# Time-mixing keys and values as three products of rounded parts instead of one fp32 product

## The chip, the cores and the metric

The kernel runs on one core of a Trainium2 chip. Its time is the device time of one execution in microseconds (us); several runs are taken and their median is given. A core has five engines that work side by side, each through its own queue of instructions in order: TensorE (PE in the profile; its weight loads are PEld) does matrix products into PSUM, VectorE (DVE), ScalarE (ACT) and GpSimd (POOL) do elementwise work, SyncE (SP) mostly issues transfers (DMA). Engines wait for each other through semaphores.

## The reference

It is one inference step of a two-layer decoder in fp32 with 1024 features. The 16 meta tokens, 1024 prompt tokens and 8 decode tokens (one new token in each of 8 sequences) go through layer 0 (a Conformer convolution module), a squared-ReLU MLP of width 4096, layer 1 (RWKV-7 time mixing), another such MLP and a final norm. The change lies in the time mixing:

```python
xx = prev - h                        # prev: the row before
xr, xw, xk, xv, xa, xg = (h + xx * x_mix[i] for i in range(6))
r, k, v = xr @ w_r, xk @ w_k, xv @ w_v          # 1024 x 1024 each
w_log = -softplus(-(w0 + tanh(xw @ w1) @ w2)) - 0.5
a = sigmoid(a0 + (xa @ a1) @ a2);  g = sigmoid(xg @ g1) @ g2
kk = (k * k_k) / norm(k * k_k)       # for each of 16 heads of 64
k = k * (1 + (a - 1) * k_a)
# for each token: S = S * decay + (S @ -kk) (kk * a)^T + v k^T;  y = S r
out = ((groupnorm(y) + sum(r * k * r_k) * v) * g) @ w_o
```

## The kernel before

**Layout.** Activations lie with features on the 128 partitions, in 8 blocks of 128 features (KT = 8), and tokens along the free dimension. The time-mixing stage works on four groups of 272, 256, 256 and 264 tokens (G1, L33).

**Two kinds of dense product.** Outside the time mixing, dense products are made of three products of rounded parts: `mm3` (L185 to L189) adds hi x hi, lo x hi and hi x lo in one PSUM bank. A part is the value rounded to the format fp32r (hi), or what the rounding left (lo). `load_w` splits a weight block of 128x1024 by one copy on ScalarE (L157) and four subtractions of 128x256 on GpSimd (L162); `split` (L138 to L141) does it for activations. In the time mixing the products of r, k and v take fp32 operands directly, one matmul where `mm3` has three.

**Order of a group.** `prepare(g)` (L773) loads the group's normalised rows, subtracts neighbours (L788, two thirds on VectorE, one third on GpSimd) and provides `mix(i, k)` (L808 to L813), one VectorE operation that makes a 128-feature block of one mixed input. `mixer_in(g)` (L822) then runs three loops over 8 column blocks p of 128 output features:

- r (from L927): 8 mixes, then for each p the product (`proj`, L848 to L854: 8 matmuls over the k-blocks), an eviction and a store to HBM;
- the narrow products of the gate (`gate`, `narrow`, L873), then k (from L944): 8 mixes, for each p the product, an eviction (L955), a square for the norm (L958), a small product that sums it (pn, L950) and the gate's second product (l_g, L892) with its eviction;
- the norm of k (`norms`), the narrow products of decay and rate (p_wa), then v (from L1043): 8 mixes, for each p the product and a long elementwise part on VectorE and ScalarE (L1053 to L1096) that reads r and k back from HBM (`fetch`, rk2), and `finish`, with small products (nn L1015, vt L998, pk L1031) and stores.

**Weights.** `col_stream` (L176) gives the 96 weight blocks (4 groups x r, k, v x 8) in the order of use, each loaded on SyncE's queue up to 4 blocks ahead of its use into a pool of 6 raw buffers (L755). Other pools: 4 wide buffers for the narrow weights (L756), 20 for the mixes (L757).

**The recurrence** over 17 chunks (the 16 meta tokens, then 64 tokens each) runs interleaved with these loops. `inverses` (L1124) reads small blocks, does 60 VectorE operations for each burst (L1135, L1136) and stores the result; `front` (A, L1176) and `chunk` (gg, bT, W, po, U, S, Y) are chains of small products with elementwise steps on VectorE, ScalarE and GpSimd (for GpSimd: clearing part of xa, and sw).

**What sets the order.** The program is written in generators: `tick` and `advance` (from L1318) move the recurrence forward by an amount (PACE, L1418) at each half block, `beside` moves the next group's `prepare` forward within v. A scheduler at build time then fixes the order of instructions on each engine, and pools with a set number of buffers add the waits: a tile can be written again only when its last reader is done.

Of the kernel before, what the change touches and what calls it, by code (L numbers as in the profile page):

```python
# [8 lines left out]
F32 = mybir.dt.float32  # L9
# [39 lines left out]
def hybrid_step(tc, x_prompt, x_sample, state_conv, state_shift, state_wkv, meta_tokens,  # L49
# [10 lines left out]
    with ctx:  # L60
        def pool(stack, name, bufs, **kw):
            return stack.enter_context(tc.tile_pool(name=name, bufs=bufs, reuse_waits="tile", **kw))
# [110 lines left out]
        def blocks_of(raw):  # L173
            return raw.rearrange("p (a b) -> p a b", a=KT)

        def col_stream(cols, ahead):  # L176

            raws = {}
            for i in range(len(cols)):
                for j in range(i, min(i + ahead + 1, len(cols))):  # L180
                    if j not in raws:
                        raws[j] = load_raw(col_src(*cols[j][:2]), (KT, P), cols[j][2])
                yield blocks_of(raws.pop(i))

        def mm3(ps, w, act, first, last):  # L185

# [19 lines left out]
        def tt(name, tag):  # L206
            return cur["tmp"].tile([P, cur["n"]], F32, name=name, tag=tag)
# [544 lines left out]
        nc.vector.tensor_scalar(omka, pvec[:, col["k_a"]:col["k_a"] + KT], -1.0, 1.0, op0=ALU.mult, op1=ALU.add)  # L752

        hnp = pool(ld, "hnp", 1)
        cur["raw"] = pool(ld, "wrawd", 6)  # L755
        wide = pool(ld, "wided", 4)  # L756
        mixp = pool(ld, "mixp", 20)  # L757
        lorap = pool(ld, "lorap", 1)
        pr = pool(ld, "pr", 1)
        def open_ep(stack, bufs, tag):  # L760
# [12 lines left out]
        def prepare(g):  # L773
# [33 lines left out]

            def mix(i, k):  # L808

                t = mixp.tile([P, N1], F32, name=nm("mx", i, k), tag="mx")  # L810
                nc.vector.scalar_tensor_tensor(t[:, :n], xx[:, k, :n], vec("x_mix", i * KT + k), hx[:, k, 1:1 + n],
                                               op0=ALU.mult, op1=ALU.add)
                return t[:, :n]  # L813

            prep[g] = mix, hx, sps if npr < n else None

        wrkv = col_stream([(w, p, f"w{s}{g}_{p}") for g in range(4)
                           for s, w in (("r", rwkv_w_r[0]), ("k", rwkv_w_k[0]), ("v", rwkv_w_v[0]))
                           for p in range(KT)], 4)
        carry = {"tail": lambda: None}  # L820

        def mixer_in(g, tick, ahead):  # L822
# [25 lines left out]
            def proj(w, act, wid, name, fill=None):  # L848
                ps = bank(nm("p", name))
                for k in range(KT):  # L850
                    nc.tensor.matmul(ps[:wid, :n], w[:, k, :], act[k], start=k == 0, stop=k == KT - 1)  # L851
                    if fill and k in (2, 5):
                        fill()
                return ps  # L854
# [737 lines left out]
```

## Time and profile before

| | us |
|---|---|
| median of 3 runs | 2863.09 |
| lowest and highest | 2858.82, 2869.78 |
| profiled execution | 2865.08 |
| its span in the profile | 2863.4 |

The mean clock granted to TensorE in the profiled execution was 0.975 of full speed. The time-mixing stage reaches from 1126 to 1850 us of the span. In the profile's rows, L851 is a line of the kernel, "x" counts records, and shapes are partitions x elements; a row of a view by lines ends with the engine's idle time before the group and what ended it. A row of the table by stretches has the start and end, the length, then for each engine its busy time and records, the granted clock, the busy share of the DMA engines and GB/s. In the chain of waits each piece is what the next one waited for. A row of the timeline has start, length, engine, line, operation, names, shapes and count.

### The profile page before, as it was taken

The page shows a single profiled execution, that of the slowest core. Times are in us where ns is not written, and L with a number is a line of the kernel's source. Part 1 is how long each engine was busy: PE and PEld are TensorE (multiplying, and loading weights), DVE is VectorE, ACT ScalarE, POOL GpSimd, SP SyncE. Part 2 cuts the span into 40 slices and gives each one's busy share as a digit, 9 for nine tenths or more (in the row PEclk, how much of TensorE's full clock was granted, in tenths as well). Part 3 has the DMA queues.
Part 4 walks back from the last instruction along what each step waited for, and adds up shares of the span by engine and source line. Part 5 has one row for each costly group of instructions (what it writes and reads, how often), then busy time and mean ns, then how long its engine had stood idle before and what let it go on. Part 6 is the DMA issues. An engine that isn't in the chain of part 4 may idle for free.

```text
span 2863.4 us, 51601 instructions
## 1 busy us (share of the span) xinstructions
PE 2756.3 (96%) x19594; PEld 2553.4 (89%) x19594; DVE 1795.2 (63%) x3618; ACT 1185.9 (41%) x2230; POOL 1436.1 (50%) x1983
## 2 busy tenths in 40 slices
PE   8999999999999899979999999979999999999998
PEld 7999999999999898858778877768889999999998
DVE  5999999995465545167455771679756764443444
ACT  5545444543364332232434643534345552222223
POOL 6677877987788774000000110265448783333332
PEclk9999999999999999989999999989999999999999
DMA  6663544454445643778768785675557742222211
GB/s 177 176 186 88 154 139 133 134 178 140 140 129 149 192 140 120 214 198 197 199 181 217 212 215 150 195 179 149 131 152 215 208 134 86 67 74 67 67 60 41
DMA packets 659270, 428.15 MB, mean 150 GB/s; under 512 B 126840, under 2 KB 609208, under 8 KB 659022
## 3 DMA queue, kind: packets, MB, share of 16 engines
q1 hardware_dynamic: 652780, 421.93, 52.1%
q10 hardware_dynamic: 6018, 2.89, 0.4%
q8 instruction: 155, 2.54, 0.4%
q14 instruction: 93, 0.76, 0.1%
q0 software_dynamic: 224, 0.03, 0.0%
HBM read 353.03 MB, written 72.66 MB: 149 GB/s over the span
## 4 chain that ended last, share of the span: by engine, by line
PE 37%; DVE 7%; POOL 5%; DMA 3%; issue 3%; ACT 1%; SPq 0%; DVEq 0%; POOLq 0%; ACTq 0%
PE ps_in L187 3%; PE ps_in L188 3%; PE ps_in L189 3%; POOL wo_lo L162 3%; PE out L187 3%; PE out L189 3%; PE out L188 3%; PE p_v L851 3%; PE p_k L851 2%; POOL wi_lo L162 2%; PE p_r L851 2%; PE A L1176 2%; DVE ni L1136 1%; DVE tt L1135 1%; PE U L1260 1%
## 5 line engine op out<-in xcount | busy, mean ns | idle before, releaser
L162 POOL TENSOR_TENSOR wo_lo<-wo_raw,wo_hi 128x256 fp32r<-128x256 f32 x736 | 563.4, 799 | 286.3 <-ACT wo_hi L157 267.4
L162 POOL TENSOR_TENSOR wi_lo<-wi_raw,wi_hi 128x256 fp32r<-128x256 f32 x640 | 490.5, 799 | 272.0 <-ACT wi_hi L157 259.7
L187 PE MATMUL out<-hh,wo_hi 128*128 128x352 f32 (+2 forms) x1536 | 502.7, 327 | 18.5 <-DVE h L340 9.3
L187 PE MATMUL ps_in<-m_h,wi_hi 128*128 128x352 f32 (+2 forms) x1536 | 498.8, 325 | 12.3 <-ACT m_h L269 11.5
L340 DVE TENSOR_TENSOR h<-h,out 128x352 f32<-128x352 f32 (+2 forms) x768 | 385.5, 509 | 188.3 <-PE out L189 187.2
L189 PE MATMUL out<-hl,wo_hi 128*128 128x352 f32 (+2 forms) x1536 | 494.8, 325 | 6.8 <-DVE hl L141 6.8
L188 PE MATMUL out<-hh,wo_lo 128*128 128x352 f32 (+2 forms) x1536 | 497.7, 324 | 0.0
L189 PE MATMUL ps_in<-m_l,wi_hi 128*128 128x352 f32 (+2 forms) x1536 | 497.0, 324 | 0.0
L188 PE MATMUL ps_in<-m_h,wi_lo 128*128 128x352 f32 (+2 forms) x1536 | 496.7, 324 | 0.0
L504 DVE SCALAR_TENSOR_TENSOR cv<-u,wdw,cv 128x352 f32<-128x352 f32 (+2 forms) x720 | 376.5, 572 | 0.7
L157 ACT CAST wi_hi<-wi_raw 128x1024 fp32r<-128x1024 f32 x160 | 168.0, 1050 | 396.5 <-PE out L189 189.0
L157 ACT CAST wo_hi<-wo_raw 128x1024 fp32r<-128x1024 f32 x184 | 192.8, 1049 | 311.5 <-PE out L189 144.1
L187 PEld LDWEIGHTS out<-hh,wo_hi 128*128 128x128 f32 x1536 | 292.2, 190 | 26.3 <-DVE h L340 13.7
L187 PEld LDWEIGHTS ps_in<-m_h,wi_hi 128*128 128x128 f32 x1536 | 290.9, 189 | 15.6 <-ACT m_h L269 11.7
L189 PEld LDWEIGHTS out<-hl,wo_hi 128*128 128x128 f32 x1536 | 291.7, 191 | 9.0 <-DVE hl L141 8.1
L188 PEld LDWEIGHTS out<-hh,wo_lo 128*128 128x128 f32 x1536 | 292.2, 190 | 1.3
L188 PEld LDWEIGHTS ps_in<-m_h,wi_lo 128*128 128x128 f32 x1536 | 290.7, 189 | 1.7
L189 PEld LDWEIGHTS ps_in<-m_l,wi_hi 128*128 128x128 f32 x1536 | 290.6, 189 | 1.8
L327 DVE SCALAR_TENSOR_TENSOR r<-ps_in,rs_m 128x352 f32<-128x352 f32 (+2 forms) x192 | 98.5, 515 | 235.7 <-PE ps_in L189 232.0
L141 DVE TENSOR_TENSOR hl<-s,hh 128x352 fp32r<-128x352 f32 (+2 forms) x192 | 143.8, 750 | 112.0 <-ACT hh L140 111.9
L329 ACT ACTIVATE s<-r 128x352 f32<-128x352 f32 (+2 forms) x192 | 93.7, 490 | 141.6 <-DVE r L327 141.3
L851 PE MATMUL p_r<-mx,wr_raw 128*128 128x256 f32 (+2 forms) x512 | 123.4, 396 | 4.1 <-DVE n L1017 4.1
(350 smaller groups left out, 4926.9 us busy)
## 6 DMA issues: line engine op xcount, KB each, us to landing
wi_raw<-in_w_mlp_in_dram SPq DMA_DIRECT2D x160, 512.0 KB, 4.0
wo_raw<-in_w_mlp_out_dram SPq DMA_DIRECT2D x160, 512.0 KB, 3.7
wr_raw<-in_rwkv_w_r_dram SPq DMA_DIRECT2D x32, 512.0 KB, 6.0
wk_raw<-in_rwkv_w_k_dram SPq DMA_DIRECT2D x32, 512.0 KB, 4.2
wv_raw<-in_rwkv_w_v_dram SPq DMA_DIRECT2D x32, 512.0 KB, 4.5
d_ab<-ab SPq DMA_DIRECT2D x32, 512.0 KB, 4.0
pg_raw<-in_conv_w_pw_dram SPq DMA_DIRECT2D x24, 512.0 KB, 4.6
pa_raw<-in_conv_w_pw_dram SPq DMA_DIRECT2D x24, 512.0 KB, 4.7
```

The source lines that it names most:

```text
L141: eng_lo.tensor_sub(lo, src, hi.bitcast(F32))
L157: nc.scalar.copy(hi[:, :a * b], raw[:, :a * b])
L162: eng_lo.tensor_sub(lo[:, cs], raw[:, cs], hi[:, cs].bitcast(F32))
L187: nc.tensor.matmul(ps, w[0], act[0], start=first, stop=False)
L188: nc.tensor.matmul(ps, w[1], act[0], start=False, stop=False)
L189: nc.tensor.matmul(ps, w[0], act[1], start=False, stop=last)
L327: nc.vector.scalar_tensor_tensor(r[:, :n], ps[:, :n], 0.0, rs[:, :n], op0=ALU.max, op1=ALU.mult)
L329: nc.scalar.activation(s[:, :n], r[:, :n], AF.Square)
L340: nc.vector.tensor_add(hv[:, 4 * i + m, :], hv[:, 4 * i + m, :], ps[:, :n])
L504: nc.vector.scalar_tensor_tensor(acc[m][:, :n], ug[:, m, j:j + n], wdw[:, m, j:j + 1], acc[m][:, :n], op0=ALU.mult, op1=ALU.add)
L851: nc.tensor.matmul(ps[:wid, :n], w[:, k, :], act[k], start=k == 0, stop=k == KT - 1)
L1176: nc.tensor.matmul(ps[:, i * 2 * P:(i + 1) * 2 * P], bk[:, j + i, :], xa[:, j + i].rearrange("p q x -> p (q x)"), start=True, stop=True)
```

## The change

In the products of k and v the fp32 matmul is replaced by `mm3`; r keeps its fp32 matmul. For this, `col_stream` splits the blocks of k and v one block ahead of their use, as `load_w` does elsewhere: a copy on ScalarE, four subtractions on GpSimd, into a new pool of two buffers for each part. `mix` for k and v writes to a temporary tile and splits it, the lo part by VectorE for even k-blocks and by GpSimd for odd ones. Pools become smaller: raw 6 to 4 (and the look-ahead 4 to 3), wide 4 to 3, mixes 20 of one kind to 10 of each of two kinds, which r's mixes use in turn.

```diff
-        def col_stream(cols, ahead):
+        def col_stream(cols, ahead, split_ahead):
 
-            raws = {}
+            raws, parts = {}, {}
             for i in range(len(cols)):
                 for j in range(i, min(i + ahead + 1, len(cols))):
                     if j not in raws:
                         raws[j] = load_raw(col_src(*cols[j][:2]), (KT, P), cols[j][2])
-                yield blocks_of(raws.pop(i))
+                for j in range(i, min(i + split_ahead + 1, len(cols))):
+                    if j not in parts:
+                        if not cols[j][3]:
+                            parts[j] = [blocks_of(raws[j])]
+                            continue
+                        hi, lo = (cur["wsp"].tile([P, 8 * P], F32R, name=cols[j][2] + q, tag="w" + q) for q in "hl")
+                        nc.scalar.copy(hi, raws[j])
+                        for c in range(0, 8 * P, 2 * P):
+                            cs = slice(c, c + 2 * P)
+                            nc.gpsimd.tensor_sub(lo[:, cs], raws[j][:, cs], hi[:, cs].bitcast(F32))
+                        parts[j] = [blocks_of(hi), blocks_of(lo)]
+                yield parts.pop(i)
...
-        cur["raw"] = pool(ld, "wrawd", 6)
-        wide = pool(ld, "wided", 4)
-        mixp = pool(ld, "mixp", 20)
+        cur["raw"] = pool(ld, "wrawd", 4)
+        cur["wsp"] = pool(ld, "wspd", 2)
+        wide = pool(ld, "wided", 3)
+        mixp = pool(ld, "mixp", 10)
...
             def mix(i, k):
 
-                t = mixp.tile([P, N1], F32, name=nm("mx", i, k), tag="mx")
+                if i == 0:
+                    t = mixp.tile([P, N1], F32, name=nm("mx", i, k), tag="m" + "hl"[k % 2])
+                else:
+                    t = tt(nm("mx", i, k), "t2")
                 nc.vector.scalar_tensor_tensor(t[:, :n], xx[:, k, :n], vec("x_mix", i * KT + k), hx[:, k, 1:1 + n],
                                                op0=ALU.mult, op1=ALU.add)
-                return t[:, :n]
+                if i == 0:
+                    return t[:, :n]
+                hi, lo = (mixp.tile([P, N1], F32R, name=nm("m" + q, i, k), tag="m" + q) for q in "hl")
+                split(hi[:, :n], lo[:, :n], t[:, :n], nc.gpsimd if k % 2 else nc.vector)
+                return hi[:, :n], lo[:, :n]
...
-        wrkv = col_stream([(w, p, f"w{s}{g}_{p}") for g in range(4)
+        wrkv = col_stream([(w, p, f"w{s}{g}_{p}", s != "r") for g in range(4)
...
-                           for p in range(KT)], 4)
+                           for p in range(KT)], 3, 1)
...
-                    nc.tensor.matmul(ps[:wid, :n], w[:, k, :], act[k], start=k == 0, stop=k == KT - 1)
+                    if len(w) == 1:
+                        nc.tensor.matmul(ps[:wid, :n], w[0][:, k, :], act[k], start=k == 0, stop=k == KT - 1)
+                    else:
+                        mm3(ps[:wid, :n], [part[:, k, :] for part in w], act[k], k == 0, k == KT - 1)
```

## The prediction

> **What bounds the kernel now.** I began with the page's totals, then cut the time-mixing stage into its projection phases, then asked of single phases which chain ends them.
>
> ```profile
> span 2863.4 us, 51601 instructions
> PE 2756.3 (96%) x19594; PEld 2553.4 (89%) x19594; DVE 1795.2 (63%) x3618; ACT 1185.9 (41%) x2230; POOL 1436.1 (50%) x1983
> POOL 6677877987788774000000110265448783333332
> ```
>
> TensorE is busy 96% of the span; GpSimd is busy over most of it, but its row has zeros in slices 16 to 21, which is where the time-mixing stage lies. So the changed products stand on the busiest engine, and GpSimd's new work falls where it idled. An average over the span does not say what a shorter product is worth, so the next view is the table by stretches, one for each k and v phase of the four groups (k0, v0, k1, v1, k2, v2, k3, v3); PE, PEld, DVE, ACT, POOL are busy us.
>
> ```profile
> 1163.80:1207.80 44.00, 44.00 (x193) 36.44 (x193) 2.01 (x2) 11.81 (x28) 0.00 (x0) 1.00 0.68 201
> 1207.80:1280.20 72.40, 56.10 (x465) 42.85 (x464) 48.59 (x119) 32.98 (x104) 6.11 (x21) 0.89 0.70 202
> 1322.90:1388.20 65.30, 61.66 (x521) 51.00 (x520) 35.06 (x99) 21.14 (x57) 4.54 (x8) 0.97 0.75 190
> 1388.20:1476.20 88.00, 86.11 (x781) 64.56 (x780) 54.12 (x119) 41.26 (x111) 8.73 (x18) 0.92 0.68 184
> 1532.40:1584.10 51.70, 51.70 (x415) 44.95 (x414) 16.53 (x33) 22.96 (x54) 3.31 (x5) 1.00 0.94 247
> 1584.10:1667.00 82.90, 80.27 (x994) 63.76 (x994) 61.64 (x143) 53.24 (x145) 9.18 (x21) 1.00 0.81 208
> 1728.30:1784.90 56.60, 56.60 (x285) 43.40 (x281) 7.38 (x17) 18.02 (x45) 2.11 (x2) 1.00 0.60 160
> 1784.90:1849.50 64.60, 64.60 (x675) 50.60 (x675) 40.85 (x84) 34.93 (x105) 16.11 (x50) 1.00 0.56 160
> ```
>
> k0, k2, k3 and v3 have TensorE busy from end to end. v0 has it idle for 16.3 us (72.40 - 56.10), v1 and v2 are nearly full but with a long busy time of VectorE. A busy TensorE may still be waiting inside a modelled end, so I take the chain of waits that ends each phase; these are its sums by line for k1, v1, k2, v2 and v3, in this order.
>
> ```profile
> by line: DVE ni L1136 17.2%; DVE tt L1135 16.9%; DMA d_p<-ni 12.1%; DMA ni<-d_n 8.4%; PE p_wa L873 5.6%; PE p_wa L872 5.6%; PE p_k L851 3.9%; PE A L1176 3.9%; DMA p<-d_p 3.6%; issue 2.9%; PE U L1260 2.7%; DVE xa L1183 2.1%; DVE sv L1290 2.0
> by line: PE p_v L851 25.3%; PE nn L1015 8.4%; DMA hx<-d_hn 6.4%; PE pk L1031 6.2%; PE A L1176 5.3%; DVE mx L811 4.8%; PE Y L1279 4.7%; PE l_w L892 4.0%; PE l_a L892 3.6%; PE pb L740 3.6%; DVE xx L788 3.3%; PE Y L1276 3.2%; PE po L1214 2.8%;
> by line: PE p_k L851 55.0%; PE p_wa L873 6.7%; PE pn L950 6.7%; PE l_g L892 6.7%; PE p_wa L872 6.7%; PE A L1176 3.3%; PE S L1269 2.1%; PE W L1244 2.1%; PE U L1260 2.1%; PE Y L1276 1.9%; PE Y L1279 1.8%; PE yn L1396 1.7%; PE bT L1237 1.7%; P
> by line: PE p_v L851 23.0%; PE A L1176 12.0%; DMA ey<-d_y 10.8%; DMA d_y<-yt 5.1%; PE l_w L892 4.0%; PE l_a L892 3.9%; PE U L1260 3.5%; PE pk L1031 3.0%; PE Y L1279 3.0%; PE bT L1237 2.7%; PE S L1269 2.6%; PE W L1244 2.6%; PE nn L1015 2.5%;
> by line: PE p_v L851 44.2%; PE pk L1031 8.0%; PE l_w L892 7.3%; PE l_a L892 7.0%; DMA d_dec<-dst 6.5%; PE A L1176 6.0%; PE nn L1015 4.8%; PE pb L740 3.3%; PE vt L998 2.9%; PE Y L1276 2.9%; PE S L1269 2.9%; PE U L1260 2.5%; PE W L1244 2.3%;
> ```
>
> In k2 the changed products are 55% of the chain, in v3 44%. In k1 they are 4%: there the recurrence's inverses (L1135, L1136, on VectorE) and the transfers beside them are the chain. v1 and v2 lie between.
>
> **The change, part by part.**
>
> **The products themselves.** A single fp32 matmul leaves two records in the trace, a product of rounded parts leaves one. The rows: sixteen records of a 256-column projection in the chain, the same at 264 columns, two single products of rounded parts at 348 columns that stand twelve products apart, and one at 256 columns with the matmul that starts behind it.
>
> ```profile
> 1557.09 3.45 PE p_k L851 x16
> 1741.98 3.56 PE p_k L851 x16
> ...
> 900.27 0.32 PE L187 MATMUL ps_in<-m_h,wi_hi 128*128 128x348 f32 x1
> 902.17 0.32 PE L187 MATMUL ps_in<-m_h,wi_hi 128*128 128x348 f32 x1
> ...
> 1589.44 0.28 PE L740 MATMUL pb<-r16l,hspread 128*128 128x256 f32 x1
> 1589.56 0.60 PE L892 MATMUL l_w<-lw,wa_raw 128*128 128x256 f32 x2
> ```
>
> So fp32 costs 2 x 3.45/16 = 431 ns a matmul at 256 columns and 445 at 264; at 272 the k0 phase gives 44.00 us / 193 records x 2 = 456. A product of rounded parts costs 1.90/12 = 158 ns at 348 columns and 120 at 256, from which 264 and 272 columns follow on a line as 123 and 127. Three of them are 360, 370 and 380, so each changed matmul gets 71, 75 or 76 ns shorter. There are 64 in each of the eight phases: 4.9 us in k0 and v0, 4.5 in k1, v1, k2 and v2, 4.8 in k3 and v3, together 37.4 us off TensorE. The 120 is the thinnest figure here. The Trainium skill, "TensorE: Matmul & The Clock Gate", section Back-to-back issue gap, gives N/2.4 + 2.5 ns for a warm isolated matmul, 109 at 256 columns, and says that the gap leaves no room for loading weights; by that the whole would be some 54 us instead of 37. The row at 348 columns is 10 ns above the formula's 148, so the rows decide and I stay with 37.4.
>
> **What of it counts.** Where TensorE is the chain I take it whole: k0 -4.9, k2 -4.5, k3 -4.8. v3 has its TensorE full, but 6.5% of its chain is a transfer: -4.0. v1: the changed products are a quarter of the chain, but the PE is full but for 1.9 us: -3.0. v2: -1.5, since VectorE has 61.6 us of the 82.9 already and gets more (below). v0 waits for reads of what was stored a phase before:
>
> ```profile
> DVE rk L1064 <- DMA rk<-d_rk: 8.2, 3, 3.9
> ```
>
> That wait does not shrink with the products: -0.8. k1: nothing, since the inverses end it. Sum so far: -23.5 us.
>
> **Splitting the weights.** 64 blocks of 128x1024, each one copy on ScalarE and four subtractions on GpSimd. The same work stands elsewhere in this kernel; beside it are the rows for the rest of what is added: an eviction of k, its square, a mix on VectorE, a subtraction of 128x256 on VectorE and one on GpSimd.
>
> ```profile
> L162 POOL TENSOR_TENSOR wo_lo<-wo_raw,wo_hi 128x256 fp32r<-128x256 f32 x736 | 563.4, 799 | 286.3 <-ACT wo_hi L157 267.4
> L157 ACT CAST wi_hi<-wi_raw 128x1024 fp32r<-128x1024 f32 x160 | 168.0, 1050 | 396.5 <-PE out L189 189.0
> L955 ACT COPY st<-p_k 128x256 f32<-128x256 f32 x16 | 5.9, 371 | 23.3 <-PE p_k L851 12.2 <-issue 7.3 <-PE l_g L892 1.9
> L958 ACT ACTIVATE sq<-p_k,pvec 128x256 f32<-128x256 f32 x16 | 7.7, 480 | 0.0
> L811 DVE SCALAR_TENSOR_TENSOR mx<-xx,pvec,hx 128x256 f32<-128x256 f32 x48 | 20.4, 472 | 1.0 <-PE p_v L851 1.0
> L141 DVE TENSOR_TENSOR r16l<-r,r16h x4: 425/430/444, 1209.4 to 1782.1; 128x256 fp32r<-128x256 f32 x2, 128x272 fp32r<-128x272 f32 x1, 128x264 fp32r<-128x264 f32 x1
> L788 POOL TENSOR_TENSOR xx<-hx x8: 784/790/914, 971.4 to 1589.0; 128x256 f32<-128x256 f32 x6, 128x272 f32<-128x272 f32 x2
> ```
>
> ScalarE gets 64 x 1.05 = 67 us, GpSimd 256 x 0.80 = 205 us. Per block GpSimd has 3.2 us of work; the tightest pace at which blocks are eaten is k0's: 24 x 0.127 + 4 records of other matmuls x 0.228 = 4.0 us. So it fits in throughput. In latency: the split of block p+2 can begin when block p's last product releases its buffers (2 of them). Then come the eviction 0.37, the square 0.48, the copy 1.05 and the first piece 0.80, together 2.7 us, against 4.0 until the first product needs it; the last piece is there after 5.1, needed at some 7.0 (three quarters into the block). The cover is thus 1.3 us for each block, TensorE's work on block p+1; whatever delays ScalarE or GpSimd by more than that is paid 64 times. In order on GpSimd stand also the recurrence's small operations, and they wait for VectorE and TensorE. Bounds: 0 (the margin holds) to +32 us (half a us for each block); I take 0 inside the phases, nearer the rows above, and keep the other end.
>
> **Raw buffers from 6 to 4, look-ahead from 4 to 3.** A raw block is now released by GpSimd rather than by TensorE, one block earlier. The loads stand on SyncE's queue ahead of reads of stored values, and in the merged order of SyncE each of those reads stands behind a load one block further on. DMA is at 201 GB/s in k0 and 247 in k2, so there is room in k0 and little in k2. Taken 0, kept -2 to +5.
>
> **Splitting the mixes.** 64 tiles: the VectorE operation stays; a copy on ScalarE (about the 0.37 of L955: 24 us), and a subtraction on VectorE (32 x 0.43 = 14 us) or GpSimd (32 x 0.79 = 25 us) come in. They are made at the start of a phase. k's stand behind the last r block and v's behind the wa narrow products (32 records, 7 us of TensorE), against 8 x 0.47 + 4 x 0.43 = 5.5 us of VectorE: hidden, 5 us a phase if that cover is gone. One thing does move: the tiles of the mix pool are halved (20 of one kind to 10 of each of two), so the next group's r mixes, which stood far ahead, now wait for the products of the last v block, and whatever stands behind them on VectorE, such as that block's own scan, waits too. Bounds 0 and the last block's length of 3.5 us, three times; I take 1.5 x 3 = +4.5 us.
>
> **What GpSimd's work does to VectorE.** Here are the two inverse operations (30 instructions of each in a burst), first while GpSimd is nearly idle, then while it is busy, with the table of all engines for both stretches above them.
>
> ```profile
> 1497.00:1536.00 39.00, 39.00 (x368) 31.96 (x367) 34.28 (x93) 15.15 (x37) 3.31 (x5) 1.00 0.72 193
> 1885.00:1976.00 91.00, 78.47 (x734) 69.06 (x731) 88.27 (x190) 42.84 (x80) 59.18 (x71) 0.91 0.55 142
> ...
> 1497.00:1536.00 39.00, 10.53 (x30) 1.00 0.72 193
> 1885.00:1976.00 91.00, 14.55 (x30) 0.91 0.55 142
> ...
> 1497.00:1536.00 39.00, 10.62 (x30) 1.00 0.72 193
> 1885.00:1976.00 91.00, 16.23 (x30) 0.91 0.55 142
> ```
>
> The 60 operations take 21.15 us with GpSimd at 8% (3.31 of 39.00) and 30.78 with it at 65%: 46% longer for 57 points of load. In k1 GpSimd will carry 8 x 3.2 + 4 x 0.79 + 4.5 = 33 us of some 65, 51%, so 43 points more: 35% of the 34.1% x 65.3 = 22.3 us that the inverses hold of k1's chain, +7.8 us as the upper end. The lower is 0, if the splits run while the inverses wait for their transfers (20% of the chain). I take +4. In the v phases VectorE has 49, 54, 62 and 41 us; GpSimd's load there rises by some 35 points, which would lengthen about 40 us in v2 by 28%, 11 us, to 75 us with the mixes, still under 83. That is why v2 is given only a third of its gain.
>
> **Sum:** -23.5 + 4.5 + 4 = -15.0 us. The profiled execution took 2865.08 us (span 2863.4), 2.0 over the median of 2863.09, so 2850.1 for it, **2848 us** at the median, 0.53% faster.
>
> **The rivals.**
>
> (1) The whole gain: TensorE is never kept waiting and the chains in v shorten as much as it does: -37, 2826 us. For it: a busy TensorE in six of eight phases. Against it: the chains of k1, v0 and v2.
>
> (2) The gain is eaten: the 37.4 us off TensorE are given back as waits for splits and mixes at the starts of phases, 8 phases x 2 us, and +8 in k1, +4.5 before r: -23.5 + 16 + 8 + 4.5 = +5, about 2868 us. For it: the margin of 1.3 us for each block. Against: GpSimd's idle slices.
>
> (3) Slower: VectorE becomes the bound. If GpSimd's operations stretch every VectorE operation with two inputs in SBUF by the 46% measured, at some 150 of the 199 us that VectorE is busy in v0, k1, v1 and v2, that is 69 us, half of it on the chain as L1135 to L1290 and L811 are in k1 and v1: +35, while k0, k2, k3 and v3 still give -18 and the r phases cost 4.5: +21, some 2884 us. It decides from the point at which over half of VectorE's stretch stands on the chain; v2, with 61.6 of 82.9, is first. It speaks for it that 30.78 is measured beside the same kind of subtraction; against, that VectorE idles 21 to 34 us in each of these phases. The Trainium skill, "SBUF — State Buffer", section SBUF: two separate sides, says that GpSimd and a VectorE operation with two SBUF inputs take a shared port pair as an exclusive lock, one blocking the other for a whole instruction. By that rule a 0.35 us operation beside pieces of 0.80 us would wait longer than the 46% measured; the trace agrees in direction, its number decides.
>
> (4) Products of rounded parts at 256 columns do not keep 120 ns in a long row, because weights must be loaded for each: at 144 ns three equal one fp32 matmul, and the change costs only: +8.5, 2872 us. That the products would not be single-pass at all is excluded by the 158 ns at 348 columns.
>
> **How the numbers follow.** Forecast (-6 to -26, that is 2837 to 2857): 0.42. Rival 1 (2821 to 2837): 0.13. Rival 2 (2857 to 2875): 0.22. Rival 3 (over 2875): 0.17. Rival 4: 0.06. A measurement of this kernel can tell about 0.5% from no change, 14.3 us: below 2848.8 and above 2877.4. Faster: half of the forecast and rival 1, 0.35. Slower: most of rival 3 and a little of rivals 2 and 4, 0.20. Same: the rest, 0.45. The range leaves out about one in ten on each side: 2826 to 2884.
>
> **What would show it.** In the changed profile the records of p_k and p_v products should start 120 to 127 ns apart (rival 4 otherwise). k0, k2 and k3 should be 39, 47 and 52 us long with TensorE full; if TensorE waits there for GpSimd's second parts, rival 2 is right. The operations of L1135 and L1136 in the groups' bursts at 0.35 us or at 0.5 tell the forecast from rival 3, as does the idle time of TensorE in v1 and v2. The chain of k1 should still name the inverses. The prediction would be wrong from the start if time moved outside this stage, whose instructions alone the merged orders of before and after show moved.

## The result, and the profile after

The changed kernel takes 2874.44 us (median of 14 runs, 2866.50 to 2887.52) where before takes 2866.97 (14 runs, 2857.65 to 2872.78): the ratio is 1.0035, 95% interval 1.0019 to 1.0051. It is slower by about 10 us by the ratio (the medians lie 7.5 us apart), where 15 us less were forecast. The profiled execution took 2866.5 us, the fastest of the fourteen, so its spans say where time moved better than how much. By these spans the first r product comes 12.6 us earlier (8.1 of it at the end of layer 0, see below, the rest in code that did not change), the stage is 8.0 us longer, and what follows it is 6.0 us longer. What follows takes between 1009 and 1034 us in the kernels of this document, with the same code, so these 6 us are not read.

The totals of the page of the changed kernel, with GpSimd's row of busy tenths:

```profile
span 2864.8 us, 53230 instructions
PE 2722.1 (95%) x20106; PEld 2555.6 (89%) x20106; DVE 1856.1 (65%) x3650; ACT 1263.7 (44%) x2358; POOL 1661.9 (58%) x2271
POOL 6677777987788773524425334645438783333332
```

TensorE has 34 us less to do (2756.3 to 2722.1), about what was forecast. GpSimd's zeros are gone, its busy time is up by 226 us. The line that matters is VectorE's: 61 us more, of which the added subtractions explain 14.

The same eight phases as in the prediction, k0, v0, k1, v1, k2, v2, k3, v3:

```profile
1154.78:1193.89 39.11, 38.97 (x258) 36.07 (x257) 5.11 (x8) 19.90 (x41) 23.93 (x33) 1.00 0.86 248
1193.89:1270.23 76.34, 51.37 (x529) 43.62 (x527) 54.03 (x116) 40.63 (x119) 28.03 (x50) 0.86 0.66 191
1312.37:1372.25 59.88, 51.89 (x483) 46.47 (x481) 44.88 (x105) 27.77 (x61) 31.50 (x42) 0.94 0.73 182
1372.25:1467.33 95.08, 84.99 (x951) 69.22 (x950) 62.86 (x124) 54.52 (x136) 34.26 (x47) 0.89 0.68 179
1526.16:1575.46 49.30, 45.98 (x455) 41.81 (x453) 19.04 (x32) 26.73 (x56) 29.51 (x38) 0.97 0.87 227
1575.46:1666.64 91.18, 83.18 (x1071) 70.72 (x1070) 66.54 (x140) 62.76 (x160) 30.67 (x45) 0.93 0.78 201
1732.19:1781.55 49.36, 49.36 (x332) 44.65 (x329) 10.96 (x22) 27.13 (x58) 27.34 (x37) 0.97 0.76 193
1781.55:1836.90 55.35, 55.35 (x663) 47.38 (x662) 42.91 (x78) 38.29 (x106) 35.78 (x71) 1.00 0.62 173
```

k0 is 4.9 us shorter, as forecast to a tenth; k1, k2 and k3 together are 15.1 shorter. v3 ends here with its last product; the prediction's row of v3 ran 8 us beyond that, and to the same point v3 took 56.6 us before, so it is 1.2 us shorter. v0, v1 and v2 are 4.0, 7.1 and 8.3 us longer, and TensorE idles in them for 25, 10 and 8 us (length less PE) where it idled 16, 2 and 3. Its granted clock is lower there too (0.93 for 1.00 in v2). VectorE's busy time is up in all eight rows. In the r phase of the third group the chain of waits was led by products before; now the inverses lead it. Before, then after:

```profile
by line: PE p_r L851 55.5%; PE A L1176 7.6%; PE p_g L873 6.5%; PE p_g L872 6.1%; PE gg L1214 4.2%; PE bT L1237 2.6%; PE U L1260 2.6%; PE Y L1276 2.4%; PE Y L1279 2.1%; PE S L1269 1.9%; PE W L1244 1.9%; PE nn L1015 1.8%; PE po L1214 1.8%; PE
```

```profile
by line: DVE tt L1157 16.0%; DVE ni L1158 14.9%; PE p_r L871 9.9%; DMA ni<-d_n 8.7%; issue 7.0%; DMA d_z<-ez 5.0%; DVE xa L1205 4.0%; PE gg L1236 2.8%; DVE nr L1206 2.2%; DVE sv L1312 2.2%; DVE mx L826 2.1%; DVE ez L1425 2.1%; SPq L1185 1.9
```

The products do what was expected of them. Two rows of the timeline in k0 stand eight products apart, 1.00 us, so a product of 272 columns takes 125 ns (127 forecast):

```profile
1156.88 0.28 PE L198 MATMUL p_k<-mh,wk_0h 128*128 128x272 f32 x1
...
1157.88 0.29 PE L200 MATMUL p_k<-ml,wk_0h 128*128 128x272 f32 x1
```

One thing moved that nobody looked for. At the end of layer 0, VectorE had 15 of the stage's mixes ahead of a step (hl, L141) for which TensorE waited; in the changed kernel it has 8, those of r. VectorE's timeline there, before, then after, then in e6 below, which has the pools of the change but splits v's mixes alone:

```profile
1110.62 6.27 DVE L811 SCALAR_TENSOR_TENSOR mx<-xx,pvec,hx 128x272 f32<-128x272 f32 x15
1116.80 0.51 DVE L141 TENSOR_TENSOR hl<-s,hh 128x348 fp32r<-128x348 f32 x1
```

```profile
1106.09 3.38 DVE L826 SCALAR_TENSOR_TENSOR mx<-xx,pvec,hx 128x272 f32<-128x272 f32 x8
1109.39 0.51 DVE L141 TENSOR_TENSOR hl<-s,hh 128x348 fp32r<-128x348 f32 x1
```

```profile
1107.99 6.27 DVE L826 SCALAR_TENSOR_TENSOR mx<-xx,pvec,hx 128x272 f32<-128x272 f32 x15
```

The step comes 2.9 us earlier after the operation ahead of the mixes, and the first r product 8.1 us earlier after the last product of that MLP's first half; r0 gives 3.6 of it back. The smaller pool is not what does it: e6 still has 15 mixes ahead, and the kernel before with a pool of 12 alone (e13 below) has 12 and gets some 3 of the 8.1 us. Every kernel here that splits k's mixes has 8. Why a split mix no longer stands ahead is not shown; it goes through a temporary tile and further operations.

### The profile page after: what moved, and what is told of

Same layout as the page of the kernel before. It is cut to its first block, busy times and chain, and to the rows that moved or that the text cites. A ratio compares the mean times of both kernels' runs of the same rounds, so it can differ in the third digit from the quotient of the medians.

```text
span 2864.8 us, 53230 instructions
## 1 busy us (share of the span) xinstructions
PE 2722.1 (95%) x20106; PEld 2555.6 (89%) x20106; DVE 1856.1 (65%) x3650; ACT 1263.7 (44%) x2358; POOL 1661.9 (58%) x2271
## 4 chain that ended last, share of the span: by engine, by line
PE 68%; DVE 13%; DMA 6%; POOL 6%; issue 3%; ACT 2%; SPq 1%; ACTq 0%; DVEq 0%; POOLq 0%
PE ps_in L198 7%; PE ps_in L200 7%; PE ps_in L199 7%; PE out L198 7%; PE out L200 7%; PE out L199 7%; POOL wo_lo L162 3%; PE p_r L871 3%; POOL wi_lo L162 2%; PE A L1198 1%; DVE cv L515 1%; DMA d_rk<-st 1%; DVE tt L1157 1%; PE ps_o L200 1%; DVE ni L1158 1%
## 5 line engine op out<-in xcount | busy, mean ns | idle before, releaser
L338 DVE SCALAR_TENSOR_TENSOR r<-ps_in,rs_m 128x352 f32<-128x352 f32 (+2 forms) x192 | 98.4, 515 | 237.4 <-PE ps_in L200 233.7
L141 DVE TENSOR_TENSOR hl<-s,hh 128x352 fp32r<-128x352 f32 (+2 forms) x192 | 136.9, 714 | 112.7 <-ACT hh L140 112.5
```

Source lines behind the costliest of these rows:

```text
L141: eng_lo.tensor_sub(lo, src, hi.bitcast(F32))
L338: nc.vector.scalar_tensor_tensor(r[:, :n], ps[:, :n], 0.0, rs[:, :n], op0=ALU.max, op1=ALU.mult)
```

## The experiments

**Theory A**: GpSimd's subtractions stretch VectorE's operations with two inputs in SBUF, and VectorE keeps TensorE waiting. It splits in two: **A1**, it is GpSimd's reading beside VectorE; **A2**, it is GpSimd's queue (the recurrence's small operations stand behind the subtractions, second parts come late). **Theory B**, the rival: the smaller pools make mixes and loads late. All results, each against runs of the kernel before on the same chip:

| kernel | median us | ratio to before | 95% interval |
|---|---|---|---|
| the change | 2874.44 | 1.0035 | 1.0019 to 1.0051 |
| e1, no second parts of weights | 2836.25 | 0.9875 | 0.9856 to 0.9894 |
| e7, GpSimd only writes | 2842.83 | 0.9917 | 0.9897 to 0.9937 |
| e3, pools alone | 2882.08 | 1.0037 | 1.0023 to 1.0051 |
| e4, pools and splits, fp32 products | 2901.64 | 1.0107 | 1.0089 to 1.0125 |
| e5, k alone | 2878.61 | 1.0038 | 1.0023 to 1.0054 |
| e6, v alone | 2864.27 | 0.9981 | 0.9966 to 0.9997 |
| e8, second parts on VectorE | 2867.60 | 0.9999 | 0.9984 to 1.0013 |
| e9, split once, in group 0 | 2861.90 | 0.9982 | 0.9967 to 0.9996 |
| e10, split in layer 0 | 2856.94 | 0.9958 | 0.9943 to 0.9974 |
| e11, the same, v alone | 2871.24 | 1.0021 | 1.0010 to 1.0032 |
| e12, e10 and mixes on VectorE | 2847.13 | 0.9933 | 0.9916 to 0.9950 |
| e16, e12 with other pools | 2851.25 | 0.9945 | 0.9931 to 0.9959 |
| e13, mix pool alone | 2865.08 | 0.9987 | 0.9971 to 1.0003 |
| e14, wide pool alone | 2864.82 | 1.0000 | 0.9983 to 1.0017 |
| e15, raw pool alone | 2874.23 | 1.0029 | 1.0016 to 1.0041 |

The order of instructions is fixed by a scheduler, so each edit also shuffles some neighbours; a difference of two or three us between kernels is not read.

### Without GpSimd's subtractions (e1)

```diff
-                        hi, lo = (cur["wsp"].tile(...) for q in "hl")
+                        hi = cur["wsp"].tile([P, 8 * P], F32R, name=cols[j][2] + "h", tag="wh")
                         nc.scalar.copy(hi, raws[j])
-                        for c in range(0, 8 * P, 2 * P):
-                            cs = slice(c, c + 2 * P)
-                            nc.gpsimd.tensor_sub(lo[:, cs], raws[j][:, cs], hi[:, cs].bitcast(F32))
-                        parts[j] = [blocks_of(hi), blocks_of(lo)]
+                        parts[j] = [blocks_of(hi), blocks_of(hi)]
```

> The changed kernel without the second parts of the weights: the 256 subtractions on GpSimd are left out and the first part of a weight block is used in the place of the second, so the number of products and their shapes stay. The results of k and v lack the weights' second parts. Theory A (GpSimd's subtractions stretch VectorE's operations with two SBUF inputs, VectorE keeps TensorE waiting in the v and r phases, and its clock falls there): the 10 us above before go and most of the gain on TensorE appears, 2845 to 2855 us where before has 2867; VectorE's busy time in the stage falls from 443 us to some 390. Theory B (the smaller pools make mixes and loads late, whatever GpSimd does): within 5 us of the changed kernel, 2870 to 2880, with the same waits for hx and g_raw on the chain.

36 us faster than before (0.0125 of 2867), 46 faster than the change (0.0160): further than theory A said (2845 to 2855), and B falls as the main cause. TensorE's work is that of the change; only GpSimd's 256 subtractions are gone.

### GpSimd busy, but without reading (e7)

```diff
-                            nc.gpsimd.tensor_sub(lo[:, cs], raws[j][:, cs], hi[:, cs].bitcast(F32))
+                            nc.gpsimd.memset(lo[:, cs].bitcast(F32), 0.0)
+                            nc.gpsimd.memset(cur["scr"], 0.0)         # 128x400
```

> The changed kernel with each weight subtraction on GpSimd replaced by two clears that only write: 128x256 of the second part and 128x400 of a scratch tile, together about the 0.8 us of a subtraction (a clear of 128x512 took 0.53 us, of 128x272 0.32). GpSimd's queue stays as full and TensorE still waits for the second parts, but GpSimd reads nothing; the second parts are zero, so k and v lack them. Theory A1 (VectorE's operations with two SBUF inputs are stretched while GpSimd reads SBUF): as without the subtractions, 2833 to 2846 us. Theory A2 (the subtractions stand ahead of the recurrence's small operations in GpSimd's queue, and TensorE waits for late pieces): as the changed kernel, 2870 to 2882.

24 us faster than before, inside A1's range. But the edit does not keep GpSimd as busy throughout. The clears of the scratch tile depend on nothing, and all 256 of them were placed between 1106 and 1277 us. Up to 1276.8 us of the span GpSimd is busy for 137.5 us of the stage's 161.7 (in the change, up to 1275, for 69.1 of 161.0); from there on for 128.3 of 531.3 (229.3 of 561.9). So the clean comparison is v0, which lies in the first part. Its rows for e1 and then for e7; the change's is the second of the eight above:

```profile
1193.55:1259.55 66.00, 49.90 (x530) 41.62 (x528) 46.08 (x109) 39.40 (x116) 7.42 (x22) 0.91 0.73 205
```

```profile
1202.44:1269.18 66.74, 49.98 (x529) 42.16 (x527) 46.37 (x117) 39.30 (x117) 51.03 (x140) 0.91 0.73 207
```

With GpSimd busy for 51 us but only writing, VectorE needs 46.4 us and the phase 66.7, as in e1 with 7 us of GpSimd; with the change's 28 us, mostly subtractions, it is 54.0 and 76.3. There A1 holds and A2 does not. The whole stage (first r product to last v product) in the table by stretches, first before, then the change, then e1, then e7:

```profile
1126.58:1841.44 714.86, 687.80 (x5680) 551.59 (x5679) 370.95 (x890) 284.40 (x757) 62.36 (x153) 0.97 0.73 197
```

```profile
1113.96:1836.86 722.90, 663.25 (x6253) 562.33 (x6252) 440.08 (x942) 366.15 (x893) 298.42 (x446) 0.95 0.74 198
```

```profile
1113.68:1807.63 693.95, 653.30 (x6253) 557.22 (x6252) 398.79 (x942) 364.94 (x893) 98.43 (x190) 0.95 0.77 206
```

```profile
1115.07:1808.25 693.18, 648.27 (x6252) 556.03 (x6252) 397.57 (x942) 365.20 (x893) 265.98 (x679) 0.96 0.77 206
```

Read VectorE's busy time (before its count, x890 or x942) and GpSimd's (the last with a count). With GpSimd busy for 298 us VectorE needs 440; with 98 it needs 399; with 266 us of which the added part only writes, 398. The same 942 operations take 41 us longer beside reads and nothing longer beside writes, and the stage is 29 us longer with the one, and as long as e1's with the other. TensorE's granted clock (0.95, 0.95, 0.96) does not explain that. By phases the change is longer than e1 by 10.3, 5.0 and 9.2 us in v0, v1 and v2 and by 7.8 in r1 to r3. Between e1 and e7 only the sum agrees so well: e7's k0 is 8.0 us longer (TensorE waits 5.1 us there for one second part, behind the early clears) and its k3 7.0 us shorter. The difference of e1 and e7 in the ratios, some 12 us, is not explained here; in the profiles 6 of them lie behind the stage.

One operation shows how it happens. In the change, VectorE's L1118 (128x512, two inputs in SBUF), first VectorE's rows and the subtractions of GpSimd that lie around them, at two places:

```profile
1400.94 0.68 DVE L1118 TENSOR_TENSOR ab<-wa,em 128x512 f32<-128x512 f32 x1
...
1436.64 1.21 DVE L1118 TENSOR_TENSOR ab<-wa,em 128x512 f32<-128x512 f32 x1
```

```profile
1399.85 2.36 POOL L192 TENSOR_TENSOR wv_3l<-wv_raw,wv_3h 128x256 fp32r<-128x256 f32 x2
...
1435.20 3.24 POOL L192 TENSOR_TENSOR wv_6l<-wv_raw,wv_6h 128x256 fp32r<-128x256 f32 x3
```

Five of these operations lie wholly beside subtractions: two take 0.68 us and three 1.21 or 1.22. With their neighbours of L1117, which have the same shape, they are eight, three at 0.68 and five at 1.21 or 1.22, none in between. GpSimd's pieces are long there as well (2.36 for two, where 0.73 each is common). Two more of L1117 begin when a subtraction has some 0.38 us left, with none behind it, and take 0.92 and 0.93. So one of the two waits until the other's instruction ends. It is not new with the change: beside the recurrence's own GpSimd product (sw) one of these operations took 1.55 us before, too. In e7 the same operation beside GpSimd's clears:

```profile
1436.03 0.69 DVE L1120 TENSOR_TENSOR ab<-wa,em 128x512 f32<-128x512 f32 x1
...
1435.47 1.05 POOL L192 MEMSET wk_0l<- 128x256 f32 x4 [0.54 <-PE p_v L200]
```

The Trainium skill, "SBUF — State Buffer", section SBUF: two separate sides, describes this: an exclusive lock, taken by whichever comes first for its whole instruction, that a VectorE operation with two SBUF inputs needs only against a GpSimd operation that reads SBUF. The trace agrees: two durations and none between where the whole operation lies beside subtractions, delays on both engines, and clears that delay nothing.

For the later groups, A2 is answered by the trace of the change. It names who waited for the subtractions, in us and times, and TensorE's share is small:

```profile
who waited for it (us, times):
  ACT st L977: 1.4, 1
  PEld p_k L199: 1.2, 3
  ACT wa L1075: 0.6, 1
```

All waits of the other engines for any work of GpSimd in the stage come to 7.9 us in the change and 5.9 in e1, against the 29 us between them.

### The pools alone, and with the splits (e3, e4)

e3 is the kernel before with this edit:

```diff
-        cur["raw"] = pool(ld, "wrawd", 6)
-        wide = pool(ld, "wided", 4)
-        mixp = pool(ld, "mixp", 20)
+        cur["raw"] = pool(ld, "wrawd", 4)
+        wide = pool(ld, "wided", 3)
+        mixp = pool(ld, "mixp", 12)
...
-                           for p in range(KT)], 4)
+                           for p in range(KT)], 3)
```

> The kernel before with the pools of the changed kernel and no splits or products of rounded parts: raw 6 to 4 with the look-ahead 4 to 3, wide 4 to 3, mixes 20 to 12 (in the changed kernel a v phase holds 16 of 20 and leaves 4 for the next r, here it holds 8 of 12 and leaves 4). Theory A: within 5 us of before, or up to 6 us faster, since the mixes no longer stand ahead of the last steps of layer 0. Theory B: 10 to 25 us slower than before, since the cost of the pools is there without any gain.

e4 is the change with its splits, which nothing uses:

```diff
-                        parts[j] = [blocks_of(hi), blocks_of(lo)]
+                        parts[j] = [blocks_of(raws[j])]
...
-                if i == 0:
-                    t = mixp.tile([P, N1], F32, name=nm("mx", i, k), tag="m" + "hl"[k % 2])
-                else:
-                    t = tt(nm("mx", i, k), "t2")
+                t = mixp.tile([P, N1], F32, name=nm("mx", i, k), tag="m" + "hl"[k % 2])
...
-                hi, lo = (mixp.tile(...) for q in "hl")
-                split(...)
-                return hi[:, :n], lo[:, :n]
+                return t[:, :n]
```

> The changed kernel with the weights of k and v split as there (64 copies on ScalarE, 256 subtractions on GpSimd), but the products as before, single fp32 products of the raw weights and the unsplit mixes; the parts are not used. Theory A: 20 to 45 us slower than before, as the stretch of VectorE is there without the shorter products. Theory B: as the kernel with the pools alone, within 5 us of it.

e3 is 11 us slower than before, which A did not expect: B has a part. e4 is 20 us slower than e3 (0.0070), as A said and B did not. So with fp32 products the pools cost 11 and the splits 20. (e4 keeps 20 buffers for mixes where e3 has 12; e13 below finds no cost in that.)

### Which pool (e13, e14, e15)

```diff
-        mixp = pool(ld, "mixp", 20)            # e13 alone
+        mixp = pool(ld, "mixp", 12)
-        wide = pool(ld, "wided", 4)            # e14 alone
+        wide = pool(ld, "wided", 3)
-        cur["raw"] = pool(ld, "wrawd", 6)      # e15, with the look-ahead 4 to 3
+        cur["raw"] = pool(ld, "wrawd", 4)
```

> The kernel before with the mix pool alone made smaller, 20 to 12; raw 6, wide 4 and the look-ahead of 4 stay. All smaller pools together cost 11 us. If the late mixes are the cost (the 4.5 us of the prediction, or more): 8 to 14 us slower than before. If the narrower weights' loads are (wide 4 to 3, raw 6 to 4): within 3 us of before, or faster by up to 8 us, the gain at the end of layer 0, where fewer mixes stand ahead of its last steps on VectorE.

> The kernel before with the wide pool alone made smaller, 4 to 3. If the narrow weights' late loads (g_raw on the changed kernel's chain in v2, 7.9%) are what the smaller pools cost: 8 to 15 us slower than before. If the raw pool is: within 3 us.

> The kernel before with the raw pool alone made smaller, 6 to 4, and the look-ahead 4 to 3. If the raw blocks' later loads are what the smaller pools cost: 8 to 15 us slower than before. If the wide pool is: within 3 us. If neither alone: the scheduler's order for the combination is the cost, and both are within 5 us.

The mix pool costs nothing (-3.7 us, the interval holds zero), the wide pool nothing, the raw pool with its look-ahead 8 us (5 to 12). The three come to 5 us where e3 has 11, each known to some 4 or 5 us. Where e15's 8 us lie I cannot show: its profiled stage is only 3 us longer than before's, no wait of TensorE stands out in it, and the stage begins 4.6 us later, after code that is the same.

### k alone, v alone (e5, e6)

```diff
-        wrkv = col_stream([(w, p, f"w{s}{g}_{p}", s != "r") for g in range(4)
+        wrkv = col_stream([(w, p, f"w{s}{g}_{p}", s == "k") for g in range(4)    # e6: s == "v"
...
-                if i == 0:
+                if i != 2:                                                        # e6: i != 3
```

> The changed kernel with three products of rounded parts for k alone; v keeps single fp32 products as r does, with the pools of the changed kernel. Theory A: the k phases keep their gain of some 18 us, the v phases lose theirs and most of the contention, so 5 to 15 us faster than before, 2852 to 2862. Theory B: v's gain is lost and the pools stay small, so 10 to 20 us slower than before.

> The changed kernel with three products of rounded parts for v alone; k keeps single fp32 products. With k alone it was 11 us slower than before. If the stretch of VectorE in the v phases is what costs most: 15 to 30 us slower than before. If costs and gains are alike in k and v: 5 to 15 us slower.

k alone is 11 us slower than before: theory A's range missed, B's (10 to 20 slower) holds it. v alone is 5 us faster, outside both of its ranges. With the same pools in both, the pools do not explain the difference. I had put the harm in the v phases, from their own splits. The inverses speak for k's. Around the first two bursts (120 operations), all engines, then L1157 and L1158, for k alone and then for v alone:

```profile
1290.00:1368.00 78.00, 66.12 (x508) 58.67 (x507) 62.47 (x158) 29.46 (x69) 28.61 (x39) 0.93 0.76 184
1290.00:1368.00 78.00, 24.51 (x60) 0.93 0.76 184
1290.00:1368.00 78.00, 25.90 (x60) 0.93 0.76 184
```

```profile
1294.00:1356.00 62.00, 60.12 (x418) 51.60 (x417) 50.93 (x151) 21.00 (x55) 5.78 (x9) 1.00 0.92 217
1294.00:1356.00 62.00, 20.40 (x60) 1.00 0.92 217
1294.00:1356.00 62.00, 20.38 (x60) 1.00 0.92 217
```

The inverses run in the r and k phases. With k's splits beside them GpSimd is busy for 28.6 us of that stretch and the 120 operations take 50.4 us; with v's splits it is 5.8 us and 40.8. Over the whole stage their 240 operations take 98.4 us with k alone and 83.1 with v alone; 94.5 in the change, 83.0 in e1, 81.6 before. They are a chain that the next chunk waits for. That their delay reaches the end, and that v's operations have more room around them, is argued, not shown: the inverses are 11 of the 41 us of VectorE's stretch in the change, and most of the time over e1 appears in v0 to v2.

### The second parts elsewhere (e8, e9, e10, e11, e12, e16)

e8 makes them on VectorE:

```diff
-                        for c in range(0, 8 * P, 2 * P):
-                            cs = slice(c, c + 2 * P)
-                            nc.gpsimd.tensor_sub(lo[:, cs], raws[j][:, cs], hi[:, cs].bitcast(F32))
+                        nc.vector.tensor_sub(lo, raws[j], hi.bitcast(F32))
```

> The changed kernel with the second parts of the weights made by VectorE, one subtraction of 128x1024 for each of the 64 blocks (an estimate from 0.43 us for 128x256 is 1.1 to 1.6 us each, 70 to 100 us in all). Theory A1: the stretch goes, VectorE's own new work about replaces it (its busy time in the stage 437 + 70 to 100, against 478 in the changed kernel), so 2855 to 2885 us. Theory A2: GpSimd's queue is free and VectorE has room in most phases, 2838 to 2855.

As before, to 0.1%, within A1's range. VectorE is busy for 475.7 us in its stage, 77 more than in e1: what the stretch took, its own work takes now.

e9 splits in group 0, stores both parts to HBM and loads them in the other groups:

```diff
+                    elif g == 0:
+                        raws[j] = load_raw(col_src(src, p), (KT, P), name)
+                    else:
+                        both_ = [blk(name + q, F32R) for q in "hl"]
+                        for q, t in enumerate(both_):
+                            nc.sync.dma_start(t.bitcast(F32), d_ws[j % (3 * KT) - KT, q])
...
+                        for q, t in enumerate((hi, lo)):
+                            nc.sync.dma_start(d_ws[j - KT, q], t.bitcast(F32))
```

> The changed kernel with the weights of k and v split only in the first group; both parts are stored to HBM there and loaded by the other three groups, from one pool of 8 blocks in the place of raw and split pools. 16 splits in the place of 64, and 24 MB more of loads and 16 MB of stores. If the subtractions cost the 41 us between the changed kernel and the one without them, wherever they stand: three quarters come back, 2842 to 2855 us. If the added transfers bind (the stage moves 198 GB/s, and up to 266 in a short stretch): waits of TensorE for the parts, and 2865 or more.

Only 5 us faster than before, between its two ranges. Its v0 is 86.4 us long, 10 more than in the change; a row of the table by stretches of that phase:

```profile
1202.00:1290.00 88.00, 61.69 (x536) 48.97 (x535) 53.78 (x120) 42.86 (x117) 30.08 (x52) 0.84 0.97 308
```

The DMA engines are 97% busy, at 308 GB/s, and the chain of waits there is led by transfers (of d_v 13.3%, the store of a second part 8.5%). That the added stores hold up the transfers that v0 waits for is likely from this, not shown.

e10 splits in the last MLP pass of layer 0 instead, where VectorE is half idle, and all groups load both parts; e11 does it for v alone.

```diff
+            def split_early():
+                for i, w in enumerate([rwkv_w_k[0], rwkv_w_v[0]]):
+                    for p in range(KT):
+                        for q, t in enumerate(load_col(w, p, f"ws{i}_{p}", nc.vector)):
+                            nc.sync.dma_start(d_ws[i * KT + p, q].rearrange("p (a b) -> p a b", a=KT), t.bitcast(F32))
+                        yield
...
+                if j % 1 == 0:                     # once for each block of the pass; e11: j % 2
+                    next(early, None)
```

> The weights of k and v are split once, in the last MLP pass of layer 0 (one first part by ScalarE and one 128x1024 subtraction by VectorE for each of 16 blocks, VectorE being half busy there), stored to HBM, and all four groups load both parts; no weight is split in the time mixing. Theory A1 (the cost is GpSimd's reading beside VectorE): nearly what the kernel without the subtractions had, less some 5 us for the work in layer 0, 2838 to 2850 us, with v0 at 66 to 70 us (76 in the changed kernel). If the doubled loads of k and v (0.5 to 1 MB a block, 32 MB more over the stage) hold TensorE up instead: waits of p_k and p_v for the parts in k0 and k2, the shortest phases, and 2855 or more.

> The same for v alone: 8 blocks split in layer 0, k keeps single fp32 products. Theory A1: with the splits gone the k phases' gain is real, so this is slower than the kernel with both, 2848 to 2860 us. If the k phases gain nothing whatever is done about GpSimd (k alone was 11 us slower than before, v alone 5 us faster): as fast as the kernel with both, or faster.

e10 is 12 us faster than before, less than A1's range, and its time lies in the range given for doubled loads that hold TensorE up. But the waits named for that are not there: TensorE is busy through all of k0's 38.7 us and never waits for a loaded part. Instead layer 0 pays for the work (its last first-half product of the MLP is at 1125 us, at 1105 to 1114 in the kernels that leave layer 0 alone). e11 is 18 us slower than e10 (0.0063), the way A1 said, though beyond its range (2848 to 2860): with no split in the stage, k's shorter products are worth their 18.7 us of TensorE.

e12 is e10 with every mix's second part on VectorE; e16 is e12 with a block pool of 7, look-ahead 2, and the wide pool of 4.

```diff
-                split(hi[:, :n], lo[:, :n], t[:, :n], nc.gpsimd if k % 2 else nc.vector)
+                split(hi[:, :n], lo[:, :n], t[:, :n], nc.vector)
```

> The kernel that splits k's and v's weights in layer 0, with the second parts of all mixes on VectorE in the place of half of them on GpSimd (32 subtractions of 0.79 us on GpSimd become 32 of 0.43 us on VectorE). Theory A1: GpSimd's last large reads in the stage go, VectorE gets 14 us and loses some stretch: within 5 us of it, rather faster. Theory A2 (GpSimd's queue): 3 to 8 us faster.

> The kernel with the splits in layer 0 and all mixes' second parts on VectorE, its block pool 8 to 7 with a look-ahead of 2 in the place of 3, and the wide pool 3 to 4. If the wide pool is what costs: 5 to 15 us faster than it, some 2832 to 2842 us. If the look-ahead of blocks is: as slow or slower, 2847 to 2865.

e12 is the fastest kernel but for the two that leave work out: 2847.13 us, 0.9933 of before (0.9916 to 0.9950). That 32 subtractions on GpSimd are worth some 7 us (e10 to e12; the intervals touch) is a little more than A1 allowed for and inside A2's 3 to 8, so it does not tell the two apart. e16 is no faster, which agrees with e14: the wide pool is not a cost.

## Why the prediction was wrong

- **The products**: right. 37.4 us off TensorE were forecast, 34 less busy time measured; 127 ns a product forecast at 272 columns, 125 measured. k0 came out at 39.1 us as forecast, k2 and k3 at 49.3 and 49.4 (47 and 52); k1, for which nothing was counted, came out 5.4 shorter. The sum of -23.5 was near: without the subtractions (e1) the stage is 20.9 us shorter than before. That the v phases gain little by themselves was right in kind: in e1 they sum to 6.4 us less than before, where 9.3 were counted, nearly all of it in v0. Rival 4 is excluded.
- **Late second parts** (0 taken, up to +32 kept; most of rival 2): right at 0. TensorE waited 1.2 us for them. The time, 2874, lies in rival 2's band (2857 to 2875), but not for rival 2's reason.
- **What GpSimd's work does to VectorE** (+4 taken, in k1 alone): this step failed, and it set the sign. The runs show +29 us in the stage (722.90 against 693.95 and 693.18), from 41 us more of VectorE; k1 has 2.0 of it, v0 to v2 have 24.6. The stretch in v2 had been worked out at 11 us (VectorE has 66.5 us there, 58.4 in e1) and then dropped, because VectorE's total still stayed below the phase's length; v2 is 9.2 us longer than in e1. That is the error: VectorE's operations there are links of chains (the inverses, the steps of v, the mixes), so a stretched link counts whether or not the engine has idle time elsewhere; 29 of 41 us came through. I had also read 46% as a mean, where the trace shows a wait for a whole instruction of the other engine. Rival 3 named this mechanism and priced it at 35, from 69 us of stretch of which half counts; measured were 41 and seven tenths, so that the price came so close is partly luck. Its sum, 2884, was 10 too high; the end of layer 0 gave back 8.1 that it did not know of.
- **Raw pool and look-ahead** (0 taken, -2 to +5 kept): too low; 8 us alone (e15), in the kernel before. Its place is open, and what it costs in the change no run shows.
- **Smaller mix pool** (+4.5): wrong; -3.7 alone (e13). The r phases are 9.8 us longer in the changed profile (r0 to r3: +3.6, -0.6, +2.6, +4.2). r0's part goes with the end of layer 0 (r0 is as long in e1, 41.2 us); the other 6.2 go with the subtractions, since e1's r1 to r3 sum to 1.5 less than before's (158.7 against 160.2). What splitting k's mixes frees at the end of layer 0, 8.1 us in the profile, was not seen at all, although the 20 mixes stood on VectorE's order. v3 was counted at -4.0 from a row that ran 8 us past its last product; it gave 1.2.
- **Outside the stage**: the 8.1 us at the end of layer 0 moved because of the change, against the forecast that all stays in the stage. The other differences there lie in code that is the same.

The parts do not add up by themselves: pools 11, splits 20 with fp32 products, and in the change 46 for the subtractions alone (e1 to the change). With shorter products the same stretch weighs more, since TensorE no longer covers it; that reading is argued, not shown.

## What to carry to other kernels

An idle engine is not free: before giving GpSimd elementwise work with reads, list VectorE's operations with two SBUF inputs that will run beside it and ask whether they are links of a chain, not whether VectorE has idle time left. Work that depends on weights alone can be done once, where its engine is free, and kept in HBM, if the stage has DMA room for it; that, with the mixes' second parts on VectorE, turned 0.35% slower into 0.67% faster here. When work that runs ahead gets another step, or its pool another size, look at which instructions then stand ahead, at both ends of the stage. When an experiment adds work to keep an engine busy, check in the trace that it ran where it was meant to.

## What the runs showed of the hardware

- GpSimd's clears (128x256 in 0.31 us) do not delay VectorE's operations with two inputs in SBUF (L1120 in e7: 0.68 to 0.69 us beside them); its subtractions of 0.73 us delay such an operation of 128x512 by up to 0.54 us (0.68 to 1.22), and pieces beside them last 1.2 us or more, up to 1.8.
- VectorE's operations with an input in PSUM kept their time beside the subtractions, here one of the recurrence, before and then after (minimum, median, maximum; after, 13 of the 68 lie beside a subtraction for most of their length and take 402 to 407 ns):

```profile
L1184 DVE TENSOR_TENSOR nr<-A,m_ar x68: 404/406/411, 1309.3 to 2104.2; 128x256 f32<-128x256 f32 x68
```

```profile
L1206 DVE TENSOR_TENSOR nr<-A,m_ar x68: 402/406/411, 1297.5 to 2103.9; 128x256 f32<-128x256 f32 x68
```

- The DMA engines moved 308 GB/s at a 97% busy share (e9, v0).
